# One hybrid S5 / retention / ConvGLU layer: up projection with the token halves swapped and its products reordered, and the S5 state stored step-major

## The chip, the cores and the metric

The kernel runs on one core of one Trainium2 chip. The metric is the device time of one execution in microseconds: three executions of the kernel before gave 2680.92, 2681.28 and 2684.0 us, median 2681.28 us. The engines are named as the profile names them: PE multiplies matrices (PEld loads its weights), DVE is the vector engine, ACT the scalar engine, POOL is GpSimd, and SP's queue issues nearly all DMAs. Each engine takes its instructions strictly in order.

## The reference, cut to what matters

```python
# 2048 tokens, 1024 channels, one layer
h   = modulate(rms_norm(x), ...)
p   = h @ w_in                       # S5 input u, and q, k, v, g of the retention
s5  = s5_readout(...)                # 32 groups x 16 channels, complex state of 64, scans in both directions
ret = retention_mixer(...)           # 4 heads, chunks of 128
x   = x + mx[2] * (concat(s5, ret) @ w_out)
hx2 = modulate(rms_norm(x), ...)

def conv_ffn(h, w_up, conv_w, conv_b, w_down):       # D_FF = 2816
    a, g = split(h @ w_up, 2)
    gp = pad(g, one token of zeros on each side)
    g_conv = conv_b + gp[:, 0:n] * conv_w[0] + gp[:, 1:n+1] * conv_w[1] + gp[:, 2:n+2] * conv_w[2]
    return (gelu(g_conv) * a) @ w_down

out = rms_norm(x + mx[5] * conv_ffn(hx2))
```

The convolution runs along the tokens, so the last token of the first half needs the gate value of the first token of the second half, and the reverse.

## The kernel before, in words

The program is written in program order, and a scheduler then sets the order on each engine; `tc.high_priority(offset=n)` moves what stands in it ahead. Tiles come from pools; a tile waits until what lay at its place is no longer used.

**Sweeps with S5 beside them.** After the S5 input is projected, 16 sweeps (two token halves, four heads, kv and qg) project k, v, q, g in units of 24 products. Between the units a generator runs S5 for four blocks of eight groups. The state of a block is the tile `X`, 128 partitions (64 states forward, 64 backward) by 8 groups, 2 parts (real, imaginary) and 288 positions: 18 chunks of 16 steps, stored as [chunk k, step j]. `s5_inj` multiplies on PE and copies into `X` with ACT (L888 to L890). `s5_scan` goes through the steps j = 1 to 15, four DVE operations each (L903 to L906) over all 18 chunks, and then through the chunks (L915 to L918). `s5_fix` adds the carries (DVE and POOL). `s5_read` copies a pair of groups into `E` with ACT (L954, L955) and multiplies on PE.

**Output projection.** 16 token tiles in the order 8, 12, 9, 13, ..., 0, 4, ..., 3, 7: the second half comes first. `out_norm` and `out_tr` normalise a tile and transpose it on PE; `blocks` forms seven combinations of the four blocks of a half, `H[0]` to `H[6]`. For the first half (hf 0), 0 to 3 go at once into SBUF, split into a high and a low part; all others go to DRAM (`Dhc`) and come back by `refill` and `refill_split`.

**Up projection.** Two halves of 1024 tokens (hf 0, then hf 1), in each 11 pairs of steps: kind 1 (gate columns `G`), kind 0 (value columns `A`), 44 steps in all. A step multiplies 2x2 blocks with seven block products; `product` issues 12 matmuls of 128x512 for one (4 of the contraction, 3 for the split into high and low parts), so a step has 84. Its products are numbered 0 to 6 here; 0, 2, 4 and 6 add up in one PSUM bank (`mm`), 1 has a bank of its own (`y`), 3 and 5 share one (`sc`). After each product a copy on ACT or an addition on DVE takes the result out, and a later product on that bank waits for it. The weights of a step come by one DMA of 1 MB into `stg` (`raw_load`, two steps ahead); `prep_a` makes the four weight blocks of products 0 to 3 and `prep_b` those of 4 to 6: sums on DVE and POOL, the high part on ACT, the low part on POOL (`split_lo`, L159). Of each of the two weight tiles there is one buffer, so the next step's can be made only after this step's products are through with it.

**The border token.** Half 0 comes first, so the gate value of token 1024 isn't there yet. Before, `out_tr` saves that token's input (`hsave`), and for each gate step of half 0 `prep_a` multiplies the raw weights with it: eight DVE operations of 128x256 (L1400, L1402), which stand ahead of the sums of `prep_a` because those overwrite the raw weights. Two small matmuls (L1525) add them up over the partitions, and the result is copied into the last column of `G`. For half 1 the last gate column of half 0 is kept in `gsv`.

**Gate and value.** `conv` runs three DVE operations of 128x1024 (L1510 to L1512) and the gelu on ACT (L1513); the kind 0 step multiplies with it (L1544) and stores `Dact`.

**Down projection.** Four groups of 512 tokens; for each of 22 blocks of rows `b_load` loads `w_down` and `Dact`, splits them (ACT L1564, DVE L159), and 24 matmuls follow.

Of the kernel before, what the change touches and what calls it, by code (L numbers as in the profile page):

```python
# [18 lines left out]
P = 128  # L19
D = 1024  # L20
# [63 lines left out]
def layer_kernel(ctx, tc, I, out, dbg=None):  # L84
# [34 lines left out]
    Dhc = [{i: dram(f"Dhc{hf}{i}", [P, 4, 512]) for i in range(7) if hf == 1 or i >= 4} for hf in range(2)]  # L119
# [747 lines left out]
    def s5_inj(b):  # L867
# [5 lines left out]
        for g4 in range(4):  # L873
# [48 lines left out]
    def s5_fix(b, X, lb, E):  # L922
        Xk = X.rearrange("p g r (k j) -> p g r k j", j=16)
        for g4 in range(4):
            go = 2 * g4
            S = lambda r: Xk[:, go:go + 2, r, 1:17, 15:16].to_broadcast([P, 2, 16, 15])
            Lp = lambda r: lb[:, go:go + 2, 17 * r:17 * r + 15].unsqueeze(2).to_broadcast([P, 2, 16, 15])
            o = lambda r: Xk[:, go:go + 2, r, 2:18, 0:15]
            fa = s_pool2.tile([P, 2, 16, 15], F32, tag="fa", name="fa")
            fb = s_pool2.tile([P, 2, 16, 15], F32, tag="fb", name="fb")  # L930
# [11 lines left out]
    def s5_read(b, X, Us):  # L942
        for g4 in range(2):
# [5 lines left out]
            for g2 in range(2):  # L949
# [9 lines left out]
                for gi in range(2):  # L959
# [3 lines left out]
                    PE.matmul(ps[:, 0:NCL], rd[:, 0, gi], E[:, gi, 0], start=False, stop=False)  # L963
                    PE.matmul(ps[:, 0:NCL], rd[:, 1, gi], E[:, gi, 1], start=False, stop=True)
# [321 lines left out]

    a2 = gp_.tile([P, 2, 8], F32, name="a2")
# [8 lines left out]
    hsave = gp_.tile([P, 8], F32, name="hsave")  # L1296
# [10 lines left out]
    def load_mix(c):  # L1307
        m = o_pool.tile([P, KT, P], F32, tag="mix", name="mix", bufs=1)
# [3 lines left out]
        x = o_pool.tile([P, D], F32, tag="x6", name="x6", bufs=2)  # L1312
# [356 lines left out]
```

## Time and profile before

| | |
|---|---|
| median of 3 executions | 2681.28 us |
| profiled execution | 2685.33 us, of it the span of instructions 2683.4 us |
| busy share of the span | PE 91%, DVE 68%, POOL 43%, ACT 35% |
| mean granted clock of PE | 0.96 of full speed |
| sweeps with S5 beside them | about 300 to 680 us |
| output projection | 1037 to 1227 us |
| up projection | 1242 to 2170 us |
| down projection | 2178 to 2683 us |

Busy time is not a bound by itself: an engine can be busy all through a stage and wait for nobody, or be idle for a moment in which everyone waits for it. The stages above have different limits, so each is read by itself: who is busy all of the time, and what released the engine that stood still.

### The profile page before, as it was taken

Reading aid. Unit: us, or ns where it says so; the run is one execution under the profiler, and the core shown is the slowest. Engines: PE = TensorE matmul, PEld = TensorE weight load, DVE = VectorE, ACT = ScalarE, POOL = GpSimd, SP = SyncE. Lnnn points to the kernel's source line nnn. Section 1 sums busy time; section 2 is a strip of 40 time slices with the busy share of each in tenths; the row PEclk is TensorE's granted clock in tenths of the full one; section 3 lists DMA queues with packets and bytes.
Section 4 is the critical chain, followed back from the end, with each engine's and each line's share of the span. In section 5 each row is a group of like instructions: output and inputs, shape, how many; then the busy total and the mean of one; then the engine's idle time right before and its main releaser. Section 6 shows DMA issues by size and latency. Waiting matters only on the chain.

```text
span 2683.4 us, 35873 instructions
## 1 busy us (share of the span) xinstructions
PE 2430.6 (91%) x12940; PEld 2056.4 (77%) x12940; DVE 1811.5 (68%) x3447; ACT 943.6 (35%) x1718; POOL 1166.9 (43%) x786
## 2 busy tenths in 40 slices
PE   7889978788999878996999999999999989999998
PEld 3679967677898867885777777778778768787876
DVE  9892599999487695567766666766666543636364
ACT  2453524343332442122333233533333332424232
POOL 2345154355343343212666675867777710303020
PEclk9899988898999989997999999999999999999999
DMA  8545533435787653754222221422222264545452
GB/s 252 190 138 153 150 99 98 116 105 177 222 273 243 193 187 120 215 159 148 83 79 71 71 79 63 148 88 79 90 68 79 79 223 142 198 147 204 142 172 91
DMA packets 334319, 377.83 MB, mean 141 GB/s; under 512 B 43942, under 2 KB 284410, under 8 KB 331838
## 3 DMA queue, kind: packets, MB, share of 16 engines
q1 hardware_dynamic: 332702, 374.98, 43.4%
q8 instruction: 102, 1.67, 0.3%
q10 hardware_dynamic: 1440, 0.56, 0.1%
q14 instruction: 75, 0.61, 0.1%
HBM read 268.00 MB, written 107.47 MB: 140 GB/s over the span
## 4 chain that ended last, share of the span: by engine, by line
PE 46%; DVE 17%; DMA 8%; issue 3%; POOL 2%; ACT 1%; SPq 1%; DVEq 0%; ACTq 0%; POOLq 0%
PE mm L1483 13%; PE sc L1483 6%; PE y L1483 3%; PE mm L154 3%; PE mm L156 3%; PE mm L155 3%; DVE mac L1402 2%; DMA stg<-in_w_up_dram 2%; PE y L154 2%; PE y L156 2%; PE y L155 2%; PE sc L154 2%; PE sc L155 2%; PE sc L156 2%; POOL w L159 1%
## 5 line engine op out<-in xcount | busy, mean ns | idle before, releaser
L159 POOL TENSOR_TENSOR w<-stg,w 128x512 fp32r<-128x512 f32 (+1 forms) x268 | 535.0, 2016 | 349.1 <-ACT w L1425 130.5
L1483 PE MATMUL mm<-hc,w 128*128 128x512 f32 x2112 | 528.3, 400 | 29.7 <-DVE G L1499 24.9
L1483 PEld LDWEIGHTS mm<-hc,w 128*128 128x128 f32 x2112 | 403.3, 192 | 125.4 <-DVE G L1499 28.8
L159 DVE TENSOR_TENSOR bw<-draw,bw 128x1536 fp32r<-128x1536 f32 x88 | 159.8, 1819 | 245.2 <-ACT bw L1564 245.0
L1483 PE MATMUL sc<-hc,w 128*128 128x512 f32 x1056 | 271.7, 396 | 21.9 <-ACT A L1496 10.4
L1483 PEld LDWEIGHTS sc<-hc,w 128*128 128x128 f32 x1056 | 198.6, 190 | 72.9 <-ACT A L1496 17.1
L1564 ACT ACTIVATE bw<-draw 128x1536 fp32r<-128x1536 f32 x88 | 130.5, 1486 | 277.7 <-PE tr L156 225.3
L804 POOL TENSOR_TENSOR ob<-ra,rb 128x128 f32<-128x128 f32 x128 | 79.8, 623 | 320.4 <-DVE rb L803 207.1
L154 PE MATMUL mm<-w,hT 128*128 128x256 f32 x688 | 208.2, 303 | 1.2 <-ACT ob L849 1.2
L156 PE MATMUL mm<-w,hT 128*128 128x256 f32 x688 | 207.0, 301 | 0.0
L155 PE MATMUL mm<-w,hT 128*128 128x256 f32 x688 | 206.2, 300 | 0.0
L1582 POOL TENSOR_TENSOR acc<-acc,tm 128x512 f32<-128x512 f32 x24 | 35.1, 1484 | 333.4 <-DVE tm L1581 325.8
L154 PEld LDWEIGHTS mm<-w,hT 128*128 128x128 f32 x688 | 135.3, 197 | 6.5 <-issue 2.6
L1483 PE MATMUL y<-hc,w 128*128 128x512 f32 x528 | 137.2, 392 | 0.0
L156 PEld LDWEIGHTS mm<-w,hT 128*128 128x128 f32 x688 | 135.0, 196 | 2.2
L155 PEld LDWEIGHTS mm<-w,hT 128*128 128x128 f32 x688 | 135.1, 196 | 2.0
L1483 PEld LDWEIGHTS y<-hc,w 128*128 128x128 f32 x528 | 99.2, 188 | 21.8
L155 PE MATMUL y<-w,hT 128*128 128x256 f32 x336 | 102.4, 305 | 0.0
L154 PE MATMUL y<-w,hT 128*128 128x256 f32 x336 | 101.4, 302 | 0.5 <-ACT ob L849 0.5
L156 PE MATMUL y<-w,hT 128*128 128x256 f32 x336 | 101.8, 303 | 0.0
L159 POOL TENSOR_TENSOR mh<-mix,mh 128x1024 fp32r<-128x1024 f32 x16 | 38.5, 2407 | 133.2 <-ACT mh L1315 108.4
L849 ACT ACTIVATE ob<-mm 128x128 f32<-128x128 f32 x86 | 23.8, 277 | 201.3 <-DVE rb L803 125.4
(466 smaller groups left out, 6429.2 us busy)
## 6 DMA issues: line engine op xcount, KB each, us to landing
stg<-in_w_up_dram SPq DMA_DIRECT2D x44, 1024.0 KB
draw<-in_w_down_dram SPq DMA_DIRECT2D x88, 512.0 KB
stg<-in_w_in_dram SPq DMA_DIRECT2D x44, 512.0 KB
Dact<-A SPq DMA_DIRECT2D x44, 512.0 KB
draw<-Dact SPq DMA_DIRECT2D x88, 256.0 KB
stg<-in_w_mod_dram SPq DMA_DIRECT2D x16, 1024.0 KB
hst<-Dhc SPq DMA_DIRECT2D x10, 1024.0 KB
wm<-in_w_mod_dram SPq DMA_DIRECT2D x8, 1024.0 KB
```

The source lines that it names most:

```text
L154: PE.matmul(ps, lh, rh, start=start, stop=False)
L155: PE.matmul(ps, lh, rl, start=False, stop=False)
L156: PE.matmul(ps, ll, rh, start=False, stop=stop)
L159: eng.tensor_tensor(lo, src, hi.bitcast(F32), op=ALU.subtract)
L804: (GP if 1 else V).tensor_tensor(dst.rearrange("p (i j) -> p i j", j=2), ta, tb, op=ALU.add)
L849: A.activation(ob[:, ch, HD:2 * HD], ps[:, HD:2 * HD], AF.Copy)
L1402: V.scalar_tensor_tensor(ac, s[:, k], hsave[:, k:k + 1], ac, op0=ALU.mult, op1=ALU.add)
L1483: PE.matmul(ps, wt[:, wl, j, k], t[:, tl, k], start=start and k == 0 and m == 0, stop=k == 3 and m == 2, skip_group_check=not start)
L1564: A.activation(w[:, 0], s, AF.Copy)
L1582: (V if g == NG - 1 else GP).tensor_tensor(ac[:, ns], ac[:, ns], tm, op=ALU.add)
```

## The change

1. The up projection takes half 1 first (`for hf in (1, 0)`), which the output projection finishes first; `blocks` puts `H[0]` to `H[3]` of half 1 into SBUF, and those of half 0 all go to DRAM.
2. The border: the eight operations and two matmuls per gate step are gone. POOL copies, out of the finished tiles, the gate columns of tokens 1024 and 1025, of token 1023, and the value column of token 1024 into a small tile `bc` (66 copies in all). For half 0 the gate of token 1024 is simply there; the activation of token 1024, which half 1 computed with a zero beside it, is computed again from `bc` for all 22 blocks at once at the end of the up projection, and `b_load` writes it over the loaded column in group 2 (22 copies of one column on DVE).
3. `up_step` takes the products in the order 0, 3, 2, 1, 4, 5, 6, with the copies and additions out of PSUM in `tc.high_priority(offset=120)`, and in the last step of half 1 refills each `H[i]` right after product i.
4. At the start, the weights of the first step are loaded one tile earlier and `prep_a(0)`, `prep_b(0)` stand before the last tile's norm and transposes. Buffers of the output pool and of the down projection are allocated at once, in another order.
5. `X` is stored as [step j, chunk k]. The copies into `X` write with a step of 18 elements; the scan's operations read and write 18 neighbours where they took every 16th element; `E` has 17 chunks of 16 (272 columns) and is read from `X` with a step of 18 elements.

```diff
@@ s5_inj
-                    A.activation(X[0:64, g, r], ps[0:64, 0:NCC], AF.Copy)
-                    A.activation(X[64:128, g, r, 0:NCX], ps[64:128, 0:NCX][:, ::-1], AF.Copy)
-                    A.activation(X[64:128, g, r, NCX:NCC], ps[64:128, NCX:NCC][:, ::-1], AF.Copy)
+                    Xg = X[:, g, r].rearrange("p (j k) -> p k j", k=18)
+                    A.activation(Xg[0:64], ps[0:64, 0:NCC].rearrange("p (k j) -> p k j", j=16), AF.Copy)
+                    A.activation(Xg[64:128, 0:2], ps[64:128, 0:NCX][:, ::-1].rearrange("p (k j) -> p k j", j=16), AF.Copy)
+                    A.activation(Xg[64:128, 2:18], ps[64:128, NCX:NCC][:, ::-1].rearrange("p (k j) -> p k j", j=16), AF.Copy)
@@ s5_scan
-        Xk = X.rearrange("p g r (k j) -> p g r k j", j=16)
+        Xk = X.rearrange("p g r (j k) -> p g r k j", k=18)
@@ s5_read
-                E = s_pool2.tile([P, 2, 2, NCL], F32, tag="E", name="E", bufs=1)
-                A.activation(E[0:64], X[0:64, g0:g0 + 2, :, NCX - 1:NCC - 1], AF.Copy)
-                A.activation(E[64:128], X[64:128, g0:g0 + 2, :, NCX - 1:NCC - 1][:, :, :, ::-1], AF.Copy)
+                E = s_pool2.tile([P, 4, NCL + 30], F32, tag="E", name="E", bufs=1)
+                Xg = X[:, g0:g0 + 2].rearrange("p g r (j k) -> p (g r) k j", k=18)[:, :, 1:18]
+                A.activation(E[0:64, :, 0:272].rearrange("p a (k j) -> p a k j", j=16), Xg[0:64], AF.Copy)
+                A.activation(E[64:128, :, 14:286].rearrange("p a (k j) -> p a k j", j=16), Xg[64:128][:, :, ::-1, ::-1], AF.Copy)
@@ blocks, steps, prep_a
-            if hf == 0 and i < 4:
+            if hf == 1 and i < 4:
-    steps = [(hf, pr, kind) for hf in range(2) for pr in range(NPR) for kind in (1, 0)]
+    steps = [(hf, pr, kind) for hf in (1, 0) for pr in range(NPR) for kind in (1, 0)]
-        if hf == 0 and kind == 1:
-            ac = gp_.tile([P, 256], F32, tag="mac", name="mac", bufs=2)
-            V.tensor_scalar(ac, s[:, 0], hsave[:, 0:1], None, op0=ALU.mult)
-            for k in range(1, KT):
-                V.scalar_tensor_tensor(ac, s[:, k], hsave[:, k:k + 1], ac, op0=ALU.mult, op1=ALU.add)
-            HALO[n] = ac
@@ the loop over the tiles of the output projection
-        if i == len(order) - 2:
+        if i == len(order) - 3:
             raw_load(0)
             raw_load(1)
+        if i == len(order) - 2:
+            prep_a(0, o_pool)
+    prep_b(0)
     finish_tile(*prev)
-    prep_a(0, o_pool)
-    prep_b(0)
@@ up_step
         product(X, w, 0, True)
-        A.activation(c11, X, AF.Copy)
-        product(Y, w, 1, True)
-        V.tensor_tensor(c11, c11, Y, op=ALU.add)
+        acopy(c11, X)
+        product(Z, w, 3, True)
+        acopy(c22, Z)
         product(X, w, 2, False)
-        A.activation(c12, X, AF.Copy)
-        product(Z, w, 3, True)
-        A.activation(c22, Z, AF.Copy)
+        acopy(c12, X)
+        product(Y, w, 1, True)
+        vadd(c11, Y)
         prep_a(n + 1, fp_)
...
@@ the loop over the steps
+                if hf == 1:
+                    GP.tensor_copy(bc[:, 1:3, fs[j]], Gs[j][:, 1:3])
+                else:
+                    GP.tensor_copy(bc[:, 0, fs[j]:fs[j] + 1], Gs[j][:, HALF:HALF + 1])
...
+                if hf == 1:
+                    GP.tensor_copy(bc[:, 3, fs[j]:fs[j] + 1], As[j][:, 0:1])
@@ b_load
+        if g == 2:
+            V.tensor_copy(s[:, D:D + 1], bc[:, 3, f:f + 1])
```

Three places show how instructions moved. The first is DVE in a gate step of the first pass of the up projection (`G` the gate tile, `y`, `sc`, `mm` the PSUM banks, `stg` the raw weights, `t` the convolution). Before:

```order
L1492 TENSOR_TENSOR G<-G,y 128x512
L1400 TENSOR_SCALAR mac<-stg,hsave 128x256
L1402 SCALAR_TENSOR_TENSOR mac<-stg,hsave,mac 128x256 x5
L1501 TENSOR_TENSOR G<-G,sc 128x512
L1402 SCALAR_TENSOR_TENSOR mac<-stg,hsave,mac 128x256
L1510 TENSOR_SCALAR t_14739<-G,colp 128x1024
L1402 SCALAR_TENSOR_TENSOR mac<-stg,hsave,mac 128x256
L1511 SCALAR_TENSOR_TENSOR t_14739<-G,colp,t_14739 128x1024
L1499 TENSOR_TENSOR G<-G,mm 128x512
```

The same place after:

```order
L1519 TENSOR_TENSOR G<-G,y 128x512
L1519 TENSOR_TENSOR G<-G,sc 128x512
L1553 TENSOR_SCALAR t_15479<-G,colp 128x1024
L1554 SCALAR_TENSOR_TENSOR t_15479<-G,colp,t_15479 128x1024
L1519 TENSOR_TENSOR G<-G,mm 128x512
```

The eight operations on `mac` ahead of and between the additions out of `sc` and `mm` are gone.

The second is PE in one step of the first pass (hc_12291, 12292, 12293 and 12294 are `H[0]` to `H[3]`, hc_14070, 14075 and 14078 are `H[4]` to `H[6]`; the last number is the weight tile). Before, one gate step:

```order
L1483 MATMUL mm<-hc_12291,w_14815 128x512 x2
L1483 MATMUL y<-hc_12292,w_14815 128x512 x2
L1483 MATMUL sc<-hc_12294,w_14815 128x512 x2
L1483 MATMUL mm<-hc_14078,w_14728 128x512 x12
L1483 MATMUL mm<-hc_12291,w_14815 128x512 x10
L1483 MATMUL y<-hc_12292,w_14815 128x512 x10
L1483 MATMUL sc<-hc_12294,w_14815 128x512 x10
L1483 MATMUL mm<-hc_12293,w_14815 128x512 x12
L1483 MATMUL sc<-hc_14075,w_14866 128x512 x12
```

After (hc_12296 to 12299 are `H[0]` to `H[3]`, hc_14063, 14062, 14061 are `H[4]`, `H[5]`, `H[6]`):

```order
L1504 MATMUL mm<-hc_12296,w_15034 128x512 x10
L1504 MATMUL y<-hc_12297,w_15034 128x512
L1504 MATMUL sc<-hc_12299,w_15034 128x512 x6
L1504 MATMUL mm<-hc_14061,w_14956 128x512 x12
L1504 MATMUL sc<-hc_12299,w_15034 128x512 x4
L1504 MATMUL mm<-hc_12298,w_15034 128x512 x12
L1504 MATMUL y<-hc_12297,w_15034 128x512 x9
L1504 MATMUL sc<-hc_14062,w_15085 128x512 x12
L1504 MATMUL mm<-hc_14063,w_15085 128x512 x12
```

Product 3 now comes before 2, product 1 after 2, and product 6 of the step before stands inside product 3.

The third is PE at the end of the output projection (`xn` to `tr` are the transposes of the normalised tiles, three tiles are left here). Before:

```order
L156 MATMUL y<-wo,mh 128x512
L1345 MATMUL tr<-cst,xn_13770 128x128 x8
L1345 MATMUL tr<-cst,xn_13887 128x128 x8
L1483 MATMUL mm<-hc_12291,w_14037 128x512 x12
L1483 MATMUL y<-hc_12292,w_14037 128x512 x12
L1345 MATMUL tr<-cst,xn_13978 128x128 x8
L1525 MATMUL tr<-cst,mac 128x1 x2
L1483 MATMUL sc<-hc_12294,w_14037 128x512 x12
```

After:

```order
L156 MATMUL y<-wo,mh 128x512
L1504 MATMUL mm<-hc_12296,w_13914 128x512 x6
L1368 MATMUL tr<-cst,xn_13782 128x128 x8
L1504 MATMUL mm<-hc_12296,w_13914 128x512 x6
L1504 MATMUL y<-hc_12297,w_13914 128x512 x12
L1368 MATMUL tr<-cst,xn_13899 128x128 x8
L1504 MATMUL sc<-hc_12299,w_13914 128x512 x12
L1504 MATMUL mm<-hc_12298,w_13914 128x512 x2
L1368 MATMUL tr<-cst,xn_13998 128x128 x8
```

The first products stand right behind the last matmul of the output projection, and the transposes of the last three tiles come between products 0, 1, 3 and 2.

## Rows read from the trace of the kernel before

**Rows 1.** Busy time by stage: start:end, length, then each engine's busy us (instructions).
```profile
core 0: us, PE busy (x) PEld busy (x) DVE busy (x) ACT busy (x) POOL busy (x), PEclk, DMA share, GB/s
...
300.00:680.00 380.00, 304.41 (x1992) 281.20 (x1991) 363.41 (x794) 142.57 (x385) 176.15 (x149) 0.91 0.41 118
...
1227.00:1298.40 71.40, 47.51 (x188) 36.33 (x188) 52.69 (x95) 26.34 (x37) 24.54 (x15) 0.81 0.37 129
1298.40:1685.15 386.75, 361.82 (x1549) 292.42 (x1549) 249.92 (x271) 127.62 (x216) 252.04 (x146) 0.98 0.22 76
1685.15:1772.40 87.25, 81.47 (x337) 65.08 (x337) 64.46 (x52) 40.32 (x53) 67.23 (x34) 0.96 0.37 132
1772.40:2129.50 357.10, 348.62 (x1513) 283.27 (x1513) 228.71 (x199) 125.09 (x198) 265.72 (x144) 1.00 0.23 80
```

**Rows 2.** Chain of waits, one pair of steps, first pass: start us, us, what.
```profile
1310.32 5.06 DMA stg<-in_w_up_dram
...
1315.40 0.83 DVE mac L1400
...
1324.97 0.61 DVE G L1499
...
1325.63 3.03 PE mm L1483 x12
...
1328.89 2.75 PE mm L1483 x12
```

**Rows 3.** Chain of waits: one recurring piece, at both ends of each pass.
```profile
1298.39 5.03 PE mm L1483 x22
...
1685.15 5.03 PE mm L1483 x22
...
1772.38 5.04 PE mm L1483 x22
...
2129.49 5.04 PE mm L1483 x22
```

**Rows 4.** Timeline, second pass: start us, us, operation, [idle before <-what released it].
```profile
1925.08 1.06 ACT L1513 ACTIVATE t<-t 128x1024 f32<-128x1024 f32 x1 [3.75 <-DVE t L1512]
...
1926.67 3.02 PE L1483 MATMUL sc<-hc,w 128*128 128x512 f32 x12 [0.94 <-ACT A L1496]
```

**Rows 5.** Timeline of PE from the output to the up projection.
```profile
1238.26 1.97 PE L1345 MATMUL tr<-cst,xn 128*128 128x128 f32 x8 [11.21 <-DVE xn L1336]
...
1258.08 1.22 PE L1483 MATMUL sc<-hc,w 128*128 128x512 f32 x2 [5.53 <-ACT w L1414]
```

**Rows 6.** Chain of waits between the two passes.
```profile
1741.97 7.73 DMA hst<-Dhc
...
1749.72 1.92 ACT hc L1469
```

**Rows 7.** Timeline from the up to the down projection.
```profile
2169.81 0.32 SPq L1545 DMA_DIRECT2D Dact<-A  x1
...
2178.24 1.22 PE L154 MATMUL mm<-bw 128*128 128x512 f32 x2 [7.70 <-ACT bw L1564]
```

**Rows 8.** Single lines on DVE: count, ns min/median/max, first and last start.
```profile
L903 DVE TENSOR_TENSOR pa<-X,lb x60: 620/656/2509, 301.1 to 613.3; 128x288 f32<-128x288 f32 x60
...
L906 DVE TENSOR_TENSOR X<-X,pb x60: 632/690/2578, 303.4 to 615.3; 128x288 f32<-128x288 f32 x60
...
L938 DVE TENSOR_TENSOR X<-X,fa x16: 644/799/1478, 366.5 to 668.5; 128x480 f32<-128x480 f32 x16
...
L404 DVE COPY PR<-ptab x2: 432/438/445, 41.2 to 42.1; 64x320 f32<-64x320 f32 x2
```

**Rows 9.** Single lines on ACT and POOL, columns as in rows 8.
```profile
L954 ACT ACTIVATE E<-X x16: 1049/1064/1067, 370.3 to 699.3; 64x1024 f32<-64x1024 f32 x16
...
L1219 ACT ACTIVATE yh<-y x32: 623/650/666, 915.5 to 1010.0; 128x256 fp32r<-128x256 f32 x32
...
L888 ACT ACTIVATE X<-sc x32: 392/403/405, 274.8 to 556.4; 64x288 f32<-64x288 f32 x32
...
L243 POOL COPY CN<-CN x2: 423/438/454, 13.0 to 20.4; 128x256 f32<-128x256 f32 x2
```

**Rows 10.** Waits from 300 to 680 us: who for whom, us, times, longest.
```profile
PEld sc L963 <- ACT E L955: 3.5, 1, 3.5
```

More of the change, by code (lines that the diff above doesn't have):

```diff
@@ L1285, in layer_kernel, with o_ct, o_hh, o_xn @@
     o_pool = Ox.enter_context(pool("o", 1, "left"))
+    def o_ct():
+        return o_pool.tile([P, 4, P], F32, tag="ct", name="ct", bufs=1)
+    def o_hh():
+        return o_pool.tile([P, KT, P], F32, tag="hh", name="hh", bufs=2)
+    def o_xn():
+        return o_pool.tile([P, D], F32, tag="xn6", name="xn6", bufs=1)
+    def o_x():
+        return o_pool.tile([P, D], F32, tag="x6", name="x6", bufs=2)
+    def o_mh():
+        return o_pool.tile([P, 2, KT, P], F32R, tag="mh", name="mh", bufs=2)
+    def o_mix():
+        return o_pool.tile([P, KT, P], F32, tag="mix", name="mix", bufs=1)
+    for mk in (o_ct, o_hh, o_xn, o_x, o_mh, o_mix):
+        mk()
     a2 = gp_.tile([P, 2, 8], F32, name="a2")
@@ L1307, in load_mix @@
     def load_mix(c):
-        m = o_pool.tile([P, KT, P], F32, tag="mix", name="mix", bufs=1)
+        m = o_mix()
         for k in range(4):
@@ L1311, in load_mix @@
             SP.dma_start(m[:, 4 + k], Dret[k][:, c * P:(c + 1) * P])
-        x = o_pool.tile([P, D], F32, tag="x6", name="x6", bufs=2)
+        x = o_x()
         SP.dma_start(x, dap(I["x"], c * P * D, [[D, P], [1, D]]))
-        mh = o_pool.tile([P, 2, KT, P], F32R, tag="mh", name="mh", bufs=2)
+        mh = o_mh()
         A.activation(mh[:, 0], m, AF.Copy)
@@ L1330, in out_norm @@
         x = MX.pop(c)[1]
-        xn = o_pool.tile([P, D], F32, tag="xn6", name="xn6", bufs=1)
+        xn = o_xn()
         ss = o_pool.tile([P, 1], F32, tag="ss6", name="ss6", bufs=2)
@@ L1339, in out_tr @@
     def out_tr(c, xn):
-        hh = o_pool.tile([P, KT, P], F32, tag="hh", name="hh", bufs=2)
+        hh = o_hh()
         for k4 in range(2):
@@ L1366, in blocks @@
         put(5, b22)
-        t3 = o_pool.tile([P, 4, P], F32, tag="ct", name="ct", bufs=1)
+        t3 = o_ct()
         V.tensor_tensor(t3, b22, b12, op=ALU.subtract)
@@ L1459, in layer_kernel @@
     hr_pool = Hr.enter_context(pool("hr", 1, "right"))
-    gsv = fp_.tile([P, NF], F32, name="gsv")
+    bc = fp_.tile([P, 4, NF], F32, name="bc")
     def refill(hf, i):
@@ L1467, in refill_split @@
     def refill_split(i, s):
-        t = hc_tile(hq_pool if i < 4 else hr_pool, i)
+        t = hc_tile(hq_pool, i) if i < 4 else H[i] if i in fresh else hc_tile(hr_pool, i)
+        fresh.discard(i)
         A.activation(t[:, 0], s, AF.Copy)
         split_lo(V, t[:, 1], s, t[:, 0])
-    ss = {i: refill(0, i) for i in (4, 5)}
+    fresh = {6, 5, 4}
+    for i in (6, 5, 4):
+        hc_tile(hr_pool, i)
+    ss = {i: refill(1, i) for i in (4, 5)}
     for i in (4, 5, 6):
@@ L1514, in conv, with next_half @@
         return t1
+    RORD = (0, 3, 2, 1, 4, 5, 6)
+    RS = {}
+    def next_half(i):
+        refill_split(i, RS.pop(i))
+        j = RORD.index(i) + 2
+        if j < 7:
+            RS[RORD[j]] = refill(0, RORD[j])
     T1 = {}
@@ L1566, in b_load, with tm_tile @@
         return w
+    def tm_tile():
+        return bp.tile([P, 512], F32, tag="tm", name="tm", bufs=2)
+    tm_tile()
     mx5 = bp.tile([P, D], F32, name="mx5")
@@ L1570, in layer_kernel, with acc_tiles @@
     ACC = {}
+    def acc_tiles():
+        for i in range(GT_):
+            ACC[i] = (bp.tile([P, D], F32, tag="acc", name="acc", bufs=2 * GT_),
+                      bp.tile([P, 2], F32, tag="ss7", name="ss7", bufs=2 * GT_))
     def down_mm(w, ps, i, n, f):
@@ L1579, in down_out @@
         ns = slice(n * 512, (n + 1) * 512)
-        tm = bp.tile([P, 512], F32, tag="tm", name="tm", bufs=2)
+        tm = tm_tile()
         V.tensor_tensor(tm, ps, mx5[:, ns], op=ALU.mult)
```

101 lines of the change are left out of this document (57 added, 44 removed).

## The prediction, as it stood before the run

> **What bounds the kernel now.** I read the stages first, then inside each stage who was waited for. In the stage table [rows 1] the reader is to look for an engine that fills its stretch: from 300 to 680 us DVE is busy 363.41 of 380 us while PE, with its clock at 0.91, is not; so the sweeps with S5 beside them are bound by DVE. In both passes of the up projection PE is nearest to full, but the two differ: nine pairs of steps lie between the first two marks of [rows 3], 1685.15 - 1298.39 = 386.76 us or 42.97 us a pair, and nine between the last two, 357.11 us or 39.68 us a pair. The same products are done in both. A product of 12 matmuls runs in 2.75 us [rows 2], 0.229 us a matmul, so a pair of 168 needs 38.5 us. The first pass loses 4.5 us a pair, the second 1.2 us.
>
> The chain of waits says where. In the first pass [rows 2] it goes from the weights' DMA (5.06 us on the chain) into the eight border operations on DVE, from there into the addition out of the `mm` bank 9.6 us after they began, and only then PE goes on: DVE's queue had the addition behind the border's work. In the second pass [rows 4] PE stands 0.94 us before product 5, which waits for ACT's copy out of the `sc` bank; that copy was queued behind a gelu for which ACT had waited 3.75 us. Then there are the joints: from the output to the up projection PE waits 11.21 us for the norm of the last tiles and 5.53 us for weights [rows 5], and the granted clock of that stretch is 0.81 [rows 1]; between the passes the refill of `H` is on the chain [rows 6]; into the down projection PE waits 7.70 us [rows 7].
>
> **The border and the order of products, steady part.** Eight DVE operations a pair and four small matmul instructions go, and with them the reason why the sums of `prep_a` had to wait. The first pass becomes what the second is, or better. In the new order products 2 and 1 (21 matmuls, 4.8 us) stand between 3 and 5, where there was product 2 alone (2.75 us), and the copies out of PSUM stand ahead of the gelu. What is late next is the weights: after product 1 has released them PE has 24 matmuls of 4 and 5 and six that need high parts alone, 6.9 us, and ACT and POOL need some 1.1 + 2.4 us for the first block. That fits. For the loss that stays I have the bounds 0 and 1.2 us a pair (the second pass as it is) and take 0.3, near the lower end, since both waits named are moved apart. Nine pairs of the first pass: 9 x (42.97 - 38.8) = -37.5 us; nine of the second: 9 x (39.68 - 38.8) = -8 us.
>
> **The border's new work.** 66 copies of one or two columns on POOL. No such copy is in the trace; from below they cost nothing, from above 0.44 us each, as the 256-column one [rows 9]: 29 us on an engine that is busy 265.72 of 357.10 us [rows 1]. They take POOL's free time, so I count 0; they are priced again among the rivals. The seven small DVE operations and one gelu at the end, and 22 one-column copies in group 2, where DVE has half of its time free: +1 us.
>
> **The joints.** From the end of the output projection (1238.26 - 11.21 = 1227.05) to the first mark of [rows 3] 71.3 us pass. By the order 162 matmuls stand there, 37.1 us, and 16 transposes, 2.0 us; so 32 us are lost. Now half 1 is first, whose last tile was finished half an output projection earlier, and the weights of products 0 to 3 are ready; products stand between the transposes. But the transposes of the last three tiles still wait for DVE's chain of norms, and PE is in order. Bounds: all 32 us gone, or none. I keep one wait of 11.2 us: -21 us. Between the passes two pairs take 87.23 us [rows 3], 77.0 at full rate: 10 us lost. The refills now run through the last step, each tile with a step's time (19 us) from its product in one pass to the next; with two buffers at 7.73 us of load, 1.92 us on ACT and as much on DVE they come every 6 us. I leave 3 us: -7 us. Into the down projection, the loads stand in SP's queue behind the store of `Dact` at 2169.81 [rows 7], which waits for product 5; that now is before product 4 and so 2.75 us earlier: -3 us.
>
> **The S5 state.** The scan has 4 x 15 x 4 = 240 operations of 288 elements. With every 16th element read they take 620 ns at least and 646 to 690 in the median [rows 8]. Operations on neighbours are shorter for their size: 480 elements in 644 ns, 320 in 438 (written with a step of 10 elements, so a step in the write cost nothing) [rows 8]. Through these two lies 1.29 ns an element, 397 ns for 288; a mean price of 420 ns leaves 0.2 us an operation, 48 us. Bounds: 0, and 240 x (0.668 - 0.397) = 65 us. DVE has almost no idle time there, so this comes off the end, as long as nothing else takes its place. What does: ACT now reads `X` for `E` with a step of 18 elements. Contiguous, 288 elements take 0.403 us and 1024 take 1.06 us, so 0.15 us fixed and 0.90 ns an element; a stepped read of only 256 takes 0.65 us [rows 9], less the fixed part 1.97 ns an element, so 1088 elements need about 2.3 us: +1.2 us for each of 32 copies, 39 us of ACT. PE waited for `E` only once, 3.5 us [rows 10], so part of it is covered; I charge 10 us. The stepped writes into `X` are not in the trace for ACT: by the DVE row they cost nothing, by ACT's stepped read 403 ns become about 710, some 40 us of ACT over 192 copies, mostly beside other work. I charge 4 us. S5 together: -48 + 14 = -34 us.
>
> The Trainium skill ("SBUF — State Buffer", Door 1: The DMA port swizzle) speaks of 16-byte lines: an access that crosses to a new line pays, so fp32 can be stepped by four elements at most for free. For the reads the rows agree (620 ns); for the write they don't (438 ns with a step of 40 bytes). By the rule both the writes into `X` and the reads for `E` would pay on ACT, and the S5 part would be the second rival below.
>
> **Sum.** -37.5 - 8 - 21 - 7 - 3 - 34 + 1 = -109.5 us against the profiled execution of 2685.3 us: 2576. The median of the runs lies 4 us below that execution: **2572 us**.
>
> **Rivals.** (1) More than I count: the scan gains 60 us and ACT hides its part, the start loses half of what I left: about 31 us less, 2541 us. For it: DVE's 17 us of idle time in 380; against it: the stretched operations (2509 ns at most in rows 8) that are no matter of layout. (2) The S5 part gives nothing: ACT with 79 us more on 142.57 us [rows 1] delays the projection's copies out of PSUM that share its queue, and PE and DVE wait for those. 2572 + 34 = 2606 us. (3) The reordered products keep 39.7 us a pair, because POOL and DVE, which stretch each other, set the pace: 20 pairs x 0.9 = 18 us given back, 2590 us. (4) The border's work was only the last of several waits: the weights' DMA or the convolution on DVE holds the first pass at 43 us a pair although the eight operations are gone. 2572 + 37.5 = 2610 us. (5) Slower: POOL's queue. Each copy for `bc` stands ahead of weight splits, and the one out of the second tile waits for product 6. Product 6 now runs inside the next step's product 3, and 25 matmuls (5.7 us) later product 5 needs the second block of `prep_b`. After product 6 come a copy out of PSUM on ACT (0.6), the copy (0.44 at most) and two splits at 1.3 to 1.75 us: 4.7 us, so 1 us of margin. If the copies come 4.5 us later than that, each of 44 steps loses 3.5 us, 154 us, and the kernel is at about 2726 us; it turns slower once a step loses 109.5 / 44 = 2.5 us. Against it: POOL idles a quarter of the pass.
>
> **Chances.** My forecast 0.53, rival (1) 0.13, (2) 0.17, (3) 0.10, (4) 0.04, (5) 0.03. Forecast with its own bounds reaches from 2555 to 2590; with (1), (2), (3) and (4) the range is 2535 to 2612 us. A difference of 0.2% is about what runs of this kernel can tell from none. Faster by more than that: 0.96, within it 0.01 (several of (2) to (4) at once and more), slower 0.03.
>
> **What would show it.** Scan operations near 420 ns, and DVE's stretch from 300 to 680 shorter by some 35 us; copies into `E` near 2.3 us; both passes at 38.5 to 39 us a pair; no wait of PE for `mac`, and the first product within 2 us of the end of the output projection with two waits for transposes after it; about 3 us lost between the passes; some 5 us of PE idle before the down projection. I am wrong if the scan's operations stay above 600 ns, if a pass is above 39.7 us a pair, or if PE's waits in the up projection name POOL.

## The result, and the profile after

The changed kernel takes **2613.45 us** (median of 4 runs, 2611.21 to 2620.0) against 2682.64 us (4 runs beside it): a ratio of 0.9746, 95% interval 0.9727 to 0.9765. It is faster by 69 us; 110 us were forecast, and 2613.45 lies just above the range given. The execution that was profiled took 2620.0 us, with a span of 2618.2 us. The ledger below is made between the two profiled spans, 2683.4 and 2618.2 us. Its stretches are cut at PE's first and last matmuls of a stage, and inside the up projection at every 84th of its 3696 matmuls (a step has 84).

| stretch | before | after | moved | forecast |
|---|---|---|---|---|
| up to the output projection (S5 is in it) | 1037.6 | 1018.5 | -19.1 | -34 |
| output projection | 188.0 | 192.0 | +4.0 | 0 |
| from its end to matmul 336 (joint, two pairs) | 116.3 | 107.3 | -9.0 | -25.2 |
| matmul 336 to 1680 (8 pairs, first pass) | 344.5 | 313.6 | -30.9 | -33.3 |
| 1680 to 2016 (between the passes) | 87.2 | 88.4 | +1.2 | -7 |
| 2016 to 3528 (9 pairs, second pass) | 357.1 | 352.8 | -4.3 | -8 |
| 3528 to the down projection | 47.5 | 44.4 | -3.1 | -3 |
| down projection | 505.2 | 501.3 | -3.9 | +1 |

(-25.2 is the start's -21 and one pair of the first pass, -37.5 / 9.)

Busy time by stretch of the changed kernel, columns as in [rows 1]:
```profile
core 0: us, PE busy (x) PEld busy (x) DVE busy (x) ACT busy (x) POOL busy (x), PEclk, DMA share, GB/s
300.00:680.00 380.00, 318.65 (x2121) 292.13 (x2119) 326.62 (x815) 212.77 (x416) 176.90 (x157) 0.96 0.44 127
1210.40:1273.40 63.00, 46.66 (x194) 36.00 (x193) 47.54 (x85) 21.54 (x28) 25.74 (x18) 0.92 0.55 184
1273.40:1631.30 357.90, 354.57 (x1514) 284.84 (x1513) 213.48 (x202) 127.01 (x199) 277.82 (x183) 1.00 0.23 81
1631.30:1719.70 88.40, 82.62 (x338) 64.95 (x336) 65.55 (x53) 40.91 (x52) 69.22 (x41) 0.96 0.38 131
1719.70:2072.50 352.80, 352.80 (x1514) 283.83 (x1512) 209.90 (x199) 125.63 (x198) 270.13 (x162) 1.00 0.23 81
```
Against [rows 1] DVE has 37 us less to do in the first stretch and is no longer full; ACT has 70 us more, which is what its stepped copies add (below). In the second pass PE is busy 352.80 of 352.80 us: there is no wait left in it, and yet it gained only 4.3 us. The reader should stop at this row: an engine without idle time can still be slower than forecast, if each of its instructions takes longer.

The chain of waits of the changed kernel, at the piece that recurs in every step (start us, us, what), with one product of 12 matmuls:
```profile
1312.25 3.26 PE mm L1504 x14
...
1625.85 3.26 PE mm L1504 x14
...
1642.65 2.80 PE sc L1504 x12
...
1714.26 3.26 PE mm L1504 x14
...
2067.06 3.26 PE mm L1504 x14
```
From 1312.25 to 1625.85 are 16 steps, from 1714.26 to 2067.06 eighteen: 19.60 us a step in both passes, 39.20 us a pair; the two pairs between take 88.4 us. This answers to [rows 3]. The product takes 2.80 us where [rows 2] had 2.75.

Single lines of the changed kernel, columns as in [rows 8]:
```profile
L904 DVE TENSOR_TENSOR pa<-X,lb x60: 445/458/2532, 307.3 to 591.4; 128x288 f32<-128x288 f32 x60
...
L907 DVE TENSOR_TENSOR X<-X,pb x60: 442/459/2546, 308.9 to 592.6; 128x288 f32<-128x288 f32 x60
...
L889 ACT ACTIVATE X<-sc x32: 639/666/707, 274.8 to 542.7; 64x288 f32<-64x288 f32 x32
...
L956 ACT ACTIVATE E<-X x16: 2072/2194/2234, 368.7 to 680.5; 64x1088 f32<-64x1088 f32 x16
...
L1582 POOL COPY bc<-G x22: 183/189/964, 1222.5 to 1657.4; 128x2 f32<-128x2 f32 x22
...
L1596 POOL COPY bc<-A x22: 178/187/2199, 1255.8 to 1681.1; 128x1 f32<-128x1 f32 x22
```
The 240 scan operations took 191.1 us together before and take 143.3 us now. The copies into `X` went from 403 to 666 ns, those for `E` from 1064 to 2194 ns [rows 9]: 192 copies into `X` take 96.0 us where they took 61.5, 32 for `E` 69.6 where they took 34.0. Of the 66 small copies on POOL 41 take 0.17 to 0.19 us, the others 0.58 to 2.2; together they are 31 us of POOL, a little more than the 29 us that the prediction put as its upper bound.

### The profile page after: what moved, and what is told of

It is laid out like the page before. It is cut to its first block, busy times and chain, and to the rows that moved or that the text cites. A ratio compares the mean times of both kernels' runs of the same rounds, so it can differ in the third digit from the quotient of the medians.

```text
span 2618.2 us, 35766 instructions
## 1 busy us (share of the span) xinstructions
PE 2421.5 (92%) x12896; PEld 2039.7 (78%) x12896; DVE 1700.4 (65%) x3387; ACT 1009.7 (39%) x1697; POOL 1189.6 (45%) x852
## 4 chain that ended last, share of the span: by engine, by line
PE 59%; DVE 20%; DMA 7%; ACT 4%; issue 4%; POOL 3%; SPq 2%; DVEq 0%; ACTq 0%; POOLq 0%
PE mm L1504 17%; PE sc L1504 9%; PE y L1504 4%; PE mm L154 4%; PE mm L155 4%; PE mm L156 4%; PE y L154 2%; PE y L155 2%; PE y L156 2%; POOL w L159 2%; PE sc L154 2%; PE sc L155 2%; PE sc L156 2%; DMA x<-in_x_dram 1%; PE tr L154 1%
## 5 line engine op out<-in xcount | busy, mean ns | idle before, releaser
L1504 PE MATMUL sc<-hc,w 128*128 128x512 f32 x1056 | 278.1, 399 | 2.3 <-POOL w L159 1.4
L804 POOL TENSOR_TENSOR ob<-ra,rb 128x128 f32<-128x128 f32 x128 | 72.8, 569 | 311.0 <-DVE rb L803 192.6
L1504 PE MATMUL y<-hc,w 128*128 128x512 f32 x528 | 150.3, 396 | 0.0
L1597 DVE TENSOR_TENSOR A<-A,t 128x1024 f32<-128x1024 f32 x44 | 78.3, 1780 | 77.0 <-ACT A L1515 40.8
L1429 ACT ACTIVATE w<-stg 128x512 fp32r<-128x512 f32 x44 | 27.8, 633 | 213.5 <-POOL stg L1427 213.5
L155 PE MATMUL y<-w,hT 128*128 128x256 f32 x336 | 102.8, 306 | 0.0
L156 PE MATMUL y<-w,hT 128*128 128x256 f32 x336 | 102.3, 304 | 0.0
```

Of the source, the lines that this page charges most:

```text
L155: PE.matmul(ps, lh, rl, start=False, stop=False)
L156: PE.matmul(ps, ll, rh, start=False, stop=stop)
L804: (GP if 1 else V).tensor_tensor(dst.rearrange("p (i j) -> p i j", j=2), ta, tb, op=ALU.add)
L1429: A.activation(w[:, 0, j], x, AF.Copy)
L1504: PE.matmul(ps, wt[:, wl, j, k], t[:, tl, k], start=start and k == 0 and m == 0, stop=k == 3 and m == 2, skip_group_check=not start)
L1597: V.tensor_tensor(As[j], As[j], T1[j], op=ALU.mult)
```

## The experiments

Each kernel was timed beside the kernel before on the same chip; where only one run is named, the reading is from its trace.

**e1: the weights 32 bytes further.** The change drops `hsave`, and with it all that lies behind it in a partition moves by 32 bytes, the weights' buffers `w16` among it. e1 puts 32 bytes there again:
```diff
+    gp_.tile([P, 8], F32, name="pad")
     Hq = ctx.enter_context(ExitStack())
```


> The changed kernel with 32 unused bytes where hsave had been, so that the weights' buffers w16 begin 38304 bytes into a partition as before, and not 38272; the order of the instructions stays. Theory A (a matmul of 512 columns takes 0.233 us instead of 0.229 because its weights begin at another place): the step of the up projection falls from 19.60 to 19.23 us, 44 steps x 0.37 = 16 us less, a ratio to the kernel before of about 0.968. Rival B (the new order of products and banks makes the matmuls longer): steps stay at 19.60 us and the ratio stays at 0.974.

Measured 2605.69 us, ratio 0.9713 (0.9698 to 0.9727). The steps take 19.23 us in both passes, the two passes together 12.7 us less, the profiled span 18.0 us less. The medians differ by 7.8 us, less than the 16 that were worked out and the 18 of the profiled spans; the runs of either kernel are 5 to 9 us apart, and the profiled execution was the fastest of e1 and the slowest of the changed kernel. The interval of the ratio leaves out rival B's 0.974, but theory A's 0.968 as well. Theory A holds for the steps, where the trace shows each one; what it is worth in time is 8 to 16 us. There is one trace of each kernel, so whether every execution has these steps is not shown.

**e9, e10, e11: the same place, other kernels and other sizes.**
The same line, in e9 in the kernel before, with 8 elements; in e10 and e11 in the changed one, with 16 and 24.

> The kernel before with 32 unused bytes ahead of w16, so that its weights begin 38336 bytes into a partition (a multiple of 64, as in the changed kernel) and nothing else. Theory A (the beginning of the weights sets how long a matmul lasts): the steps of the up projection without a wait go from 19.23 to 19.60 us, 44 x 0.37 = up to 16 us slower, ratio 1.006. Rival L (a row of matmuls falls into one of two rhythms when PE starts again after a wait, whatever the place of the weights): 19.23 us in most steps of both passes, or both values in one run, ratio within 0.002 of 1.

> The changed kernel with 64 unused bytes: weights at 38336, a multiple of 64 again. Theory A: steps of 19.60 us in both passes as in the changed kernel. Rival L: 19.23 in at least one of the passes as likely as not.

> The changed kernel with 96 unused bytes: weights at 38368, 32 bytes off a multiple of 64, as in e1. Theory A: steps of 19.23 us in both passes. Rival L: either.

e9: 2694.72 us, ratio 1.0043 (1.0029 to 1.0057), so slower by 10.6 us, where up to 16 were worked out, with the same instructions as the kernel before. Its undisturbed steps take 19.61 us. e10 (one run, 2616.63 us): 19.60 us a step. e11 (one run, 2594.41 us): **19.04 us**, a price that neither theory had. The chain of waits shows it on products of 12 matmuls; e9:
```profile
1825.83 2.80 PE mm L1484 x12
```
and e11:
```profile
1804.36 2.72 PE mm L1505 x12
```
| `w16` begins at | remainder by 128 | us a matmul | in |
|---|---|---|---|
| 38272 | 0 | 0.2333 | changed, e3, e4 |
| 38304 | 32 | 0.2289 | before, e1, e2, e5, e7, e8, e12, first pass of e6 |
| 38304 | 32 | 0.2333 | second pass of e6 (below) |
| 38336 | 64 | 0.2333 | e9, e10 |
| 38368 | 96 | 0.2267 | e11, e13, e14, e15 |

The tiles of `H` begin at a remainder of 96 in all of them, so the shortest matmul is where weights and tokens begin at the same remainder. That this is the rule wasn't tried (`H` was never moved). That the place of the weights matters is shown, by e9 without any part of the change and by the same price in every trace of a place but one; that it sets the price alone is not, as e6 shows. Why the place matters, no run tells.

**e2: the S5 part alone**, the kernel before with `s5_inj`, `s5_scan`, `s5_fix` and `s5_read` of the change.

> The kernel before with the S5 part alone (X as [step, chunk], E as changed). Theory C (ACT's stepped writes into X and stepped reads for E take back about half of what the scan gains): 15 to 19 us less than before, a ratio of 0.993 to 0.9945, steps of the up projection as before. Rival D (the S5 part by itself gives the 34 us that were forecast, and what is missing was lost to the up projection's part, by other places of buffers): ratio 0.987.

Measured 2665.64 us, ratio 0.9939 (0.9922 to 0.9956): 15 us less in all, and the output projection begins 19.6 us earlier. Theory C; the up projection isn't where the S5 term was lost.

**e3 and e4: let ACT walk neighbours.** e3 changes only the order in which ACT's three copies into `X` run over the elements; e4 also keeps `E` by step and chunk (cut here: the tile itself, the backward half, the readout's matmul and the gelu):
```diff
-  Xg = X[:, g, r].rearrange("p (j k) -> p k j", k=18)
-  A.activation(Xg[0:64], ps[0:64, 0:NCC].rearrange("p (k j) -> p k j", j=16), AF.Copy)
+  Xg = X[:, g, r].rearrange("p (j k) -> p j k", k=18)
+  A.activation(Xg[0:64], ps[0:64, 0:NCC].rearrange("p (k j) -> p j k", j=16), AF.Copy)
...
-  A.activation(E[0:64, :, 0:272].rearrange("p a (k j) -> p a k j", j=16), Xg[0:64], AF.Copy)
+  A.activation(E[0:64, :, 1:16], Xg[0:64, :, 0:15, 2:18], AF.Copy)
+  A.activation(E[0:64, :, 0], Xg[0:64, :, 15, 1:17], AF.Copy)
```


> The changed kernel with the three copies into X walked step by step: ACT writes neighbours and reads PSUM with a step of 16 elements. Theory C: a read of PSUM with a step costs ACT nothing (the copy out of PSUM into ub, 256 elements with a step of 8, took 377 ns, a contiguous one of 256 took 367), so the copies of 288 elements fall from 664 to about 400 ns, ACT has some 34 us less to do, and the kernel gets 8 to 15 us faster than the changed one: ratio to before 0.969 to 0.9715. Rival E (with the scan shorter, PE or DVE's other work set the pace of that stretch, whatever ACT does): copies of 400 ns, but within 3 us of the changed kernel, 0.974.

> As the one before, and E also kept by step and chunk: ACT's copies into E walk neighbours in runs of 16, PE reads U with a step of 16 elements for the readout, and the gelu reads PSUM with a step and writes Y5 in order. Theory C: the copies for E fall from 2.19 us to 1.0 + 0.2 us, 32 times 1 us less of ACT, another 2 to 8 us of the kernel: ratio to before 0.967 to 0.970. Rival E: nothing more than the one before gave. If PE's stepped read of U is dear, its 64 matmuls for the readout take longer than 0.46 us and some of it is lost.

e3: 2601.24 us, ratio 0.9701 (0.9679 to 0.9722); e4: 2599.41 us, 0.9689 (0.9669 to 0.971). Single lines, e3:
```profile
L889 ACT ACTIVATE X<-sc x32: 392/403/406, 274.0 to 525.4; 64x288 f32<-64x288 f32 x32
```
and e4, the copies for `E` and the readout's matmul of `U`:
```profile
L956 ACT ACTIVATE E<-X x16: 997/1010/1014, 362.9 to 661.0; 64x960 f32<-64x960 f32 x16
...
L967 PE MATMUL tr<-U,M x32: 590/607/628, 344.0 to 661.2; 128*128 128x256 f32 x32
```
The write into `X` is back at 403 ns although PSUM is now read with a step of 16 elements, and the output projection begins at 1004.1 us in e3 and at 1000.1 in e4, 14.3 and 18.3 us earlier than in the changed kernel. Theory C, against E, for e3. By their times e4 can't be told from e3. The step has moved to PE in e4: its 64 matmuls with `U` take 607 ns where they took 379, 15 us of busy time on PE. Of the 4 us by which e4's trace is ahead of e3's, its output projection gives 2.3 back (193.0 us, 190.7 in e3).

**e5: the products in the old order**, with e1's bytes, the border's work left where the change put it.
```diff
+        product(Y, w, 1, True)
+        vadd(c11, Y)
+        done(1)
+        product(X, w, 2, False)
+        acopy(c12, X)
+        done(2)
         product(Z, w, 3, True)
         acopy(c22, Z)
         done(3)
-        product(X, w, 2, False)
-        acopy(c12, X)
-        done(2)
-        product(Y, w, 1, True)
-        vadd(c11, Y)
-        done(1)
```


> The kernel of e1 (changed, with the 32 bytes) with the products of a step again in the order 0, 1, 2, 3, 4, 5, 6, and the tiles of H refilled in that order; the border's work stays at the end. Theory F (the order of the products removed the wait for the sc bank that stood in the second pass of the kernel before, the border's move removed the rest): steps in pairs of 39.7 us in both passes instead of 38.45, 20 pairs x 1.2 = 24 us more than e1, ratio to before about 0.980. Rival G (all of the gain of the passes comes from the border's work, the order gives nothing): pairs stay at 38.5 us and the ratio at 0.971.

Measured 2634.99 us, ratio 0.9817 (0.98 to 0.9833): 39.8 us a pair in the first pass, 39.7 in the second. PE's timeline has the wait of [rows 4] again:
```profile
1915.14 3.03 PE L1505 MATMUL sc<-hc,w 128*128 128x512 f32 x12 [0.95 <-ACT A L1516]
```
Theory F: of the first pass's gain the order is 1.4 us a pair (39.84 to 38.45 in e1), and the rest of the change 3.2 (43.06 to 39.84). That these 3.2 are the border's work is read from the waits, since the operations on `mac` are gone from the chain; no run puts that work back alone. In the second pass (39.68 before, 39.69 in e5, 38.45 in e1) all of the gain is the order's.

**e6: the copies for the border on DVE** instead of POOL, with e1's bytes (`GP.tensor_copy` into `bc` becomes `V.tensor_copy`, three lines).

> The kernel of e1 with the 66 small copies into bc on DVE instead of POOL. Theory H (between the passes POOL's queue stands 5.5 us behind such a copy, which waits for DVE's addition into A, and the weights' splits behind it hold PE): the stretch between the passes (from matmul 1680 to matmul 2016 of the up projection) falls from 86.6 to about 82 us; passes unchanged at 19.23 us a step: about 5 us less than e1, ratio 0.9695. Rival I (DVE's splits of the refilled tiles are what is late there, and POOL's copy only waits for the same addition): the stretch stays at 86 to 87 us.

Measured 2606.4 us, ratio 0.9707 (0.9684 to 0.973); between the passes 88.1 us. Theory H fails: POOL's queue does stand behind such a copy, but with the copies on DVE the stretch isn't shorter. Rival I's number is near; its mechanism is taken up in e12. Something else came to light, in the chain of waits: both prices of a product at one place of the weights, 2.75 us throughout the first pass and 2.80 throughout the second.
```profile
1514.53 2.75 PE sc L1505 x12
...
1799.86 2.80 PE mm L1505 x12
```
The switch comes at a restart of PE after waits, with the granted clock just back (0.57 from 1698 to 1701 us, 1.00 after that). The restart before it, at 1659.87 us, changed nothing. So a row of matmuls has more than one rhythm at a remainder of 32; why it changed there stays open.

**e12: between the passes without DVE's splits**, with e1's bytes.
```diff
-        split_lo(V, t[:, 1], s, t[:, 0])
+        if i not in done_once:
+            done_once.add(i)
+            split_lo(V, t[:, 1], s, t[:, 0])
```
(Cut here: the set `done_once`, which starts with 0 to 3, and `t = H[i]` in place of a new tile.)

> The kernel of e1 without DVE's splits of the seven tiles of H refilled between the passes (their low parts stay those of the first pass; DMA and ACT's copies of the high parts stay). Theory M (these splits delay the convolution on DVE, the gelu on ACT waits for it, and the first weights of the next step wait behind the gelu): the stretch from matmul 1680 to 2016 falls from 86.6 us to 82 us or less. Rival N (ACT's seven copies of 1.9 us or the refill's DMA do it): it stays above 85 us.

One run, 2595.53 us. The stretch falls to 77.5 us. Busy time by stretch, e1:
```profile
1624.10:1710.60 86.50, 80.75 (x337) 64.71 (x336) 65.56 (x52) 40.39 (x51) 67.43 (x40) 0.96 0.38 130
```
and e12:
```profile
1624.40:1701.90 77.50, 77.22 (x337) 62.95 (x336) 47.24 (x45) 40.22 (x51) 59.98 (x40) 1.00 0.41 147
```
DVE has 18 us less to do, ACT as much as before, and PE runs through at full clock: its four waits, 5.8 us together in e1, are down to one of 0.3, and the clock is no longer 0.96. Theory M, so far as that the splits on DVE cause the loss; ACT's copies and the DMA of rival N are all still there. One way that it goes can be followed in the timeline of the changed kernel:
```profile
1655.98 2.29 DVE L159 TENSOR_TENSOR hc<-hst,hc 128x2048 fp32r<-128x2048 f32 x1 [0.97 <-ACT hc L1487]
...
1663.65 1.28 DVE L1555 SCALAR_TENSOR_TENSOR t<-G,colp,t 128x1024 f32<-128x1024 f32 x1
...
1664.96 1.06 ACT L1556 ACTIVATE t<-t 128x1024 f32<-128x1024 f32 x1 [3.34 <-DVE t L1555]
1665.93 1.90 ACT L1487 ACTIVATE hc<-hst 128x2048 fp32r<-128x2048 f32 x1
1667.74 1.04 ACT L1425 ACTIVATE w<-stg 128x1024 fp32r<-128x1024 f32 x1
...
1668.83 0.73 PE L1504 MATMUL mm<-hc,w 128*128 128x512 f32 x2 [0.97 <-ACT w L1425]
...
1672.56 6.95 PE L1504 MATMUL mm<-hc,w 128*128 128x512 f32 x22 [2.48 <-POOL w L159]
```
A split of 2.29 us puts the convolution back, ACT stands 3.34 us before its gelu, the next step's first weights (`w`, L1425) stand behind the gelu and a refill's copy, and PE waits for them. A second way isn't told apart from this one: two of PE's four waits name POOL, and POOL's own splits of the weights are shorter in e12. POOL's timeline, e1 and then e12:
```profile
1674.41 11.15 POOL L159 TENSOR_TENSOR w<-stg,w 128x512 fp32r<-128x512 f32 x4
...
1670.12 4.60 POOL L159 TENSOR_TENSOR w<-stg,w 128x512 fp32r<-128x512 f32 x3 [0.35 <-ACT w L1441]
```
That is 2.8 us a split while DVE's splits run, and 1.5 without them. How the nine us divide between the two ways is not shown.

**e7, e8, e13: put together.** e7 is e1, e4 and e6; e8 lets the norm of the last tile write into another buffer; e13 is e8 with 96 bytes:
```diff
-        xn = o_xn()
+        xn = o_mix().rearrange("p k q -> p (k q)") if c == 7 else o_xn()
```


> e1, e4 and e6 together: weights 32 bytes further, X and E walked by neighbours, bc's copies on DVE. If the three are independent: from the changed kernel's 2613 us, 16 + 14 + 4 us less, some 2577 us, a ratio to before of 0.961; under rival I of e6 0.963.

> e7, and the norm of the last tile of the output projection writes into the buffer of mix instead of xn, so that its square need not wait for the transposes of the tile before. Theory J (the one buffer of xn holds the last transposes): PE's second wait for xn at the start of the up projection (2.9 us in e1) goes, and the start, from the end of the output projection to matmul 336, falls from 106.8 to about 104 us. Rival K (what sets that start are the weights of the second step, which come through stg after the first step's splits on POOL): the wait for xn goes, PE waits for the weights instead, and the start stays at 106 to 107 us.

> e8 with 96 bytes instead of 32 ahead of w16. If the place of the weights acts by itself, as in e11 against e1: steps of 19.04 us in place of 19.23, 44 x 0.19 = 8 us less than e8: about 2575 us, ratio 0.959. If the two rhythms come by chance at a restart, it stays at e8's 2583 us.

e7: 2585.1 us, 0.9633 (0.9616 to 0.965), which is the 0.963 of e6's rival I. e8: 2583.15 us, 0.962 (0.96 to 0.9641), by its time not to be told from e7. **e13: 2574.87 us, 0.9598 (0.9577 to 0.9618)**, the lowest median of all, 39 us under the changed kernel, and the 2575 us that were expected if the place acts by itself; its 0.2267 us a matmul held through both passes. Its interval overlaps that of e8, so the gain over e8 rests on the steps in the trace. In e8 the start falls by 4.0 us against e7 (106.5 to 102.5 us), as theory J has it. What is left is a wait for weights, but not for those that K named: PE waits for product 3 of the first step. DVE's, ACT's and PE's timelines in e8:
```profile
1207.01 0.69 DVE L1427 TENSOR_TENSOR ct<-stg 128x512 f32<-128x512 f32 x1
...
1207.74 0.63 ACT L1434 ACTIVATE w<-ct 128x512 fp32r<-128x512 f32 x1 [7.40 <-DVE ct L1427]
...
1208.42 1.22 PE L1509 MATMUL sc<-hc,w 128*128 128x512 f32 x2 [9.31 <-ACT w L1434]
```
The sum `ct` for that product stands in DVE's queue among the norms.

**e14: the first weights one tile earlier**, **e15: one refilled tile split on POOL**, both on e13.

> e13, and the first step's weights are loaded and summed one tile of the output projection earlier. Theory O (with the norm's wait gone, the start of the up projection is held by DVE's two sums for the first weights, which stand in its queue behind the last norms): the start falls from about 101.5 to 93 to 97 us, ratio 0.956. Rival P (the last two sets of transposes, which PE meets in order, set it all the same): 100 us or more, another wait for xn in place of the one for the weights.

> e13, and the first of the seven refilled tiles split on POOL instead of DVE. Theory M (DVE's splits delay the convolution): the stretch between the passes falls by 2 to 4 us. Rival: POOL's splits of the weights, which come right behind, are late instead, and the stretch stays at 85 to 88 us.

e14: 2582.07 us, 0.9626 (0.9604 to 0.9647), no better than e13: the start takes 106.8 us (103.3 in e13) and the output projection 197.2 (192.5). Rival P, as its timeline of PE has it:
```profile
1213.87 1.97 PE L1373 MATMUL tr<-cst,xn 128*128 128x128 f32 x8 [9.61 <-DVE xn L1364]
```
e15: 2577.12 us, 0.9606 (0.959 to 0.9622), not to be told from e13; the stretch between the passes is 89.5 us (87.7 in e13), though the split (4.63 us on POOL) is off DVE. The rival, in that the stretch isn't shorter: the work only changes places.

## Why the prediction was wrong, step by step

The ledger stays 44 us behind the forecast: 16.2 at the start, 14.9 in S5, 8.2 between the passes, 6.1 in the two passes, 4.0 in the output projection; the rest is 5.0 better than forecast.

**The S5 state: -34 forecast, -19.1 measured.** The scan's gain came out as forecast, 48 us of DVE, with 47.8 measured. That is in part luck: both prices were taken low, 620 ns for a median of 666 before and 420 for 453 after, and the difference stayed. What failed is "this comes off the end, as long as nothing else takes its place", with the charges of 10 us for ACT's stepped reads and 4 us for its stepped writes: of the 48 us 29 didn't reach the end, instead of 14. The read was sized right (2.3 us forecast, 2.19 measured), the write too by its upper bound (710 ns, measured 666); wrong was how much of these 70 us of ACT other work would hide (the writes stood as "mostly beside other work"). e3 and e4 show ACT's share: without the steps the output projection begins 18.3 us earlier, so they cost about 18 us and not 14, the writes alone 14 and not 4. The other 10 us of the scan's gain are missing in e4 too. Of the 340 us from 300 to 640 us DVE is idle for 14 before, for 39 in the changed kernel and for 22 in e4 (columns as in [rows 1], in this order):
```profile
300.00:640.00 340.00, 272.48 (x1767) 251.74 (x1766) 325.82 (x728) 132.28 (x359) 144.74 (x122) 0.91 0.41 117
...
300.00:640.00 340.00, 284.35 (x1903) 261.76 (x1901) 301.35 (x762) 196.81 (x389) 154.70 (x136) 0.96 0.43 124
...
300.00:640.00 340.00, 297.28 (x1977) 269.40 (x1975) 317.86 (x794) 147.90 (x417) 164.95 (x148) 0.95 0.46 132
```
So a shorter scan no longer has DVE as the only limit; what holds it in e4 was not tried and stays open. The rule that the prediction weighed for this (the Trainium skill, "SBUF — State Buffer", Door 1: The DMA port swizzle: an access that crosses to a new 16-byte line pays) is what ACT shows in both directions, 403 to 666 ns written and 1064 to 2194 ns read (1088 elements instead of 1024); the prediction let a DVE row of 438 ns stand as the lower bound for ACT's write, and charged near it. A price goes with its engine.

**The passes: a term that wasn't there.** The border's eight operations and the order of products did what was said of them (e5), the waits of [rows 2] and [rows 4] are gone, and not even the 0.3 us a pair that were left as residual are lost. What failed is "0.229 us a matmul, so a pair of 168 needs 38.5 us": that price was taken as fixed, but with `hsave` gone the weights begin elsewhere and a matmul takes 0.2333 us, 39.20 us a pair. Over 44 steps this is 44 x 0.37 = 16 us; part of it falls in the start and between the passes. e1 shows 12.7 us of it in the 34 steps of the two passes (7.8 us by the medians), and e9 that it needs neither the order nor the border's work. The two passes miss by 6.1 us only because two errors work against each other: 17 pairs x 0.7 = 12 us of price, less the 17 x 0.3 = 5 us that were charged as residual and not lost.

**The start: -21 forecast; -9.0 with two pairs, where -25.2 were due.** The first product does begin with the last matmul of the output projection, and the wait that was kept at 11.2 us is there, in two parts; but other waits weren't counted. PE's timeline:
```profile
1225.61 1.97 PE L1368 MATMUL tr<-cst,xn 128*128 128x128 f32 x8 [8.61 <-DVE xn L1359]
...
1235.66 1.79 PE L1368 MATMUL tr<-cst,xn 128*128 128x128 f32 x8 [4.00 <-DVE xn L1359]
...
1242.32 0.74 PE L1504 MATMUL mm<-hc,w 128*128 128x512 f32 x2 [1.63 <-ACT w L1425]
...
1285.70 3.48 PE L1504 MATMUL mm<-hc,w 128*128 128x512 f32 x10 [3.33 <-POOL w L159]
```
With 12.6 us for the norm, 7.1 more go, up to matmul 336, to five waits for weights and for tiles of `H`; the two longest are shown above. A further 5 us, by estimate, are clock: 0.92 granted in the first 63.0 us (0.08 x 63). The step that failed is "I keep one wait of 11.2 us". "The weights of products 0 to 3 are ready" was wrong too. The raw weights of the first two steps were asked for at 954 and 962 us and didn't hold anything up, but the weights made from them are late: DVE does the sum for product 3 of the first step only behind the norm, and the next step's sum, at 1216.51 us, stands ahead of it. DVE's timeline of the changed kernel:
```profile
1224.80 0.75 DVE L1359 TENSOR_SCALAR xn<-x,rsy 128x1024 f32<-128x1024 f32 x1
1225.46 0.68 DVE L1422 TENSOR_TENSOR ct<-stg 128x512 f32<-128x512 f32 x1
```
In the changed kernel this is hidden behind the norm's wait; in e8, where the norm is earlier, it is the wait that is left. e8 and e14 show that norm and sums share DVE's queue there: where one was put ahead, the other was late. To put the first step's sums ahead of the next step's was not tried.

**Between the passes: -7 forecast, +1.2 measured.** What failed is "I leave 3 us": at 0.2333 us a matmul the stretch needs 78.4 us, so 10.0 are lost, as many as before. None of PE's four waits there names the DMA or a tile of `H`, so "each tile with a step's time" held; what it left out is DVE's queue, in which seven splits of 2.29 us stand among the convolution's operations (e12: 9 us without them).

**What held.** Into the down projection -3.1 for -3. POOL's 66 copies cost nothing in the passes although they take 31 us, against rival (5): in the second pass PE has no wait. Rival (2) was half right, rival (3) named a dearer pair, 39.7 us, for another reason than the one that made it 39.2. The output projection's +4.0 was in no term and stays open: in the changed kernel's variants it takes 189.3 to 193.0 us and in e9, which has nothing of the change, 189.1, so traces differ by some us here. In e14, with the first weights' sums inside it, it takes 197.2. Nor was the down projection's -3.9 tried apart: it lies between 498.6 and 504.1 us in the changed kernel's variants, 504.4 in e2.

## What to carry to other kernels

When a layout is turned for one engine, price the same tile's other readers and writers on their own engines, and look whether the step can be put on the PSUM side of a copy: here that was worth 14 us at the end of the stage, for four lines. When a change adds or drops a tile, look whether buffers behind it move: compare the duration of an unchanged instruction before anything else is explained. Work taken off a full engine comes off the end only until another engine is waited for: look which one is next. Work that is spread over a stretch in which the engine has time free still delays what is behind it in an in-order queue; ask who waits for that, not how busy the engine is.

## What the runs showed of the hardware that was not expected

A matmul of 512 columns whose weights change every time takes 0.2267, 0.2289 or 0.233 us at full granted clock, and the place at which the weights' buffer begins in a partition goes with it, 32 bytes making the difference (table above). The Trainium skill ("TensorE: Matmul & The Clock Gate", Step-by-step: what each phase is for) says that loading the next weights takes no read bandwidth from the running matmul, since each has its own port; from that alone one would not expect the place to matter, and here up to 2.9% go with it; whether the loading of the weights is the reason, no run shows. At a remainder of 32 one run had two rhythms, 2.75 and 2.80 us for twelve, each kept for a whole pass.

ACT reads PSUM with a step of 16 elements at the price of neighbours (403 ns for 288 elements), while a write to SBUF with a step of 18 costs 666 and a read of 1088 costs 2194. PE's read of `U` with a step of 16 elements takes 607 ns for 256 columns instead of 379, and the next matmul starts after 414 ns instead of 215.
